# Moving two sets of loads in a one-core encoder layer: the memories behind the mixer's first output weights, the attention projection's loads behind those of the heads

## The chip, the core and the metric

The kernel runs on one NeuronCore of a Trainium2 chip. The core has a matrix engine (TensorE; PE in the profile, and PEld for its weight loads), a vector engine (VectorE; DVE), a scalar engine (ScalarE; ACT), a general engine (GpSimd; POOL) and a queue engine (SyncE; SP) that does little but issue DMA transfers between the device's memory and the on-chip buffer. The metric is device microseconds of the whole program, from launch to end, as a median of several runs.

## What is computed

One layer of an encoder, for two groups of tokens that share their weights: a sample group S (512 tokens) and a prompt group P (256 tokens), each token 1024 numbers wide, everything in fp32. The layer has four parts; each ends with a residual sum and a layer norm:

```python
x = layer_norm(DN_ALPHA * x + 0.5 * swiglu(x, ffn1_w_gu, ffn1_w_down), ...)
x = layer_norm(DN_ALPHA * x + parallel_mixer(x, ...), ...)          # ends with  merged @ w_out
x = layer_norm(DN_ALPHA * x + memory_cross_attention(x, mem, w_q, w_kv, w_o), ...)
x = layer_norm(DN_ALPHA * x + 0.5 * swiglu(x, ffn2_w_gu, ffn2_w_down), ...)

def memory_cross_attention(x, mem, w_q, w_kv, w_o):
    q = (x @ w_q).reshape(B, T, 4, 256)
    k, v = jnp.split(mem @ w_kv, 2, axis=-1)                        # mem: 256 vectors for each group
    s = jnp.einsum('bthd,bmhd->bhtm', q, k) * (256 ** -0.5)
    o = jnp.einsum('bhtm,bmhd->bthd', jax.nn.softmax(s, axis=-1), v)
    return o.reshape(B, T, 1024) @ w_o
```

The change touches the seam between the mixer and the attention, and the end of the attention.

## The kernel before, in words

**Products in three parts.** Every fp32 operand is split by `split` (L83) into a high part, copied by ScalarE (L84), and a low part, the difference, made by VectorE (L85). A product is then three matmuls (L103, L104, L105: high by high, high by low, low by high).

**Weights.** `load_w` (L87) loads 128x1024 of weights (512 KB) through the SP queue (L93) into a `raw` tile, and splits it into `wh` and `wl`. The pool has three `raw` places and five of each of `wh` and `wl`. A load therefore waits until one of the three raw places has been split, and a split until one of the five weight places has been used up.

**The seam.** The mixer's last matmuls are those of its second branch (`pt<-oT`, traced by `branch`, L1019, with VectorE's `put_gla`, L1032). Then `attention` (L1082) begins, in this order of the program:

- It opens three pools, among them `mem` for the split memories `mh` and `ml`. That pool takes over space of pools that the mixer's end has just closed.
- L1099 to L1104, four times: both groups' memories, two transfers of 256 KB (L1102), into a `raw` tile of the same three places; then a split into `mh` and `ml`. The memories are first used much later, by `keys_values` (L1110).
- `tok_out` (L1055) for the mixer's output product: six groups of token tiles and halves of the columns, three groups for the first half, then the same three for the second. A group uses four weight tiles, each loaded the first time it is needed (L1063), and makes matmuls named `to`. Between the weights of the first groups `tok_out` can call hooks: it takes one list of functions from `hooks` after each weight tile (L1070).
- Norms, transposes (`lt`), the keys and values into DRAM (`kd`, `vd`), and the queries, which are made with a seven-product scheme (`products`, L488) from sums of the inputs held in a pool `sums`, staged in a pool `qs` and stored to DRAM (`qd`) by ScalarE's queue (L1228).

**The heads.** `fetch` (L1200) loads q (1536 KB), k and v (1024 KB each) of a head through SP (L1212). Heads 0 and 2 have their q and k in a pool `even`, heads 1 and 3 in a pool `odd`; each pool has one place for q and one for k, so q and k of head 2 wait until the scores of head 0 have been made, and those of head 3 until the scores of head 1 have. There are two places for v. `odd` is opened after `qs` and `sums` have been closed and takes their space. For each head there are `scores` (matmuls `sc`, then the softmax), `probs_T` (transposes `pT`) and `values` (matmuls `ov`).

**The projection.** A second `tok_out` (L1320) multiplies by `w_xo`. It loads eight weight tiles (L93; all but the first five go into a pool that is opened by a hook), and its hooks make the last head's values, bring the residual back (`x2_back`, L1303: six loads of 512 KB, L1305) and load the norm's parameters. After that comes the second feed-forward part.

**What sets the order.** The engines run their instructions in a fixed order that is made when the kernel is compiled. The scheduler goes through a planned time; of the instructions that it holds ready at a moment, it puts the one that stands earliest in the program next on its engine. On the chip each engine then keeps that order: an SP transfer that waits holds up all SP transfers behind it, whether they could go or not. `tc.issue_after(ins)` adds a rule for the order alone: what is traced in the block on the engine of `ins` comes behind `ins` on that engine. It adds no wait.

Of the kernel before, what the change touches and what calls it, by code (L numbers as in the profile page):

```python
# [7 lines left out]
F32 = mybir.dt.float32  # L8
# [33 lines left out]
S = Stream("S", TS, 0)  # L42
P = Stream("P", TP, TS)
# [12 lines left out]
def _encoder(ctx, tc, nc, io, out, dbg):  # L56
# [6 lines left out]
    def psum(name):  # L63
        return pp.tile([128, 512], F32, tag="ps", name=name)
# [13 lines left out]
    def nid(p):  # L78
        uid[0] += 1
        return f"{p}{uid[0]}"  # L80


    def split(hi, lo, src, lo_eng=None):  # L83
        nc.scalar.activation(hi, src, AF.Copy)  # L84
        (lo_eng or nc.vector).tensor_tensor(lo, src, hi.bitcast(F32), op=ALU.subtract)  # L85

    def load_w(src, lo_eng=None, pool=None, in_parts=False, extra=1):  # L87

        raw = wp.tile([128, 1024], F32, tag="raw", bufs=3, name=nid("raw"))
        h = (pool or wp).tile([128, 1024], F32R, tag="wh", bufs=extra if pool else 5, name=nid("wh"))  # L90
        l = (pool or wp).tile([128, 1024], F32R, tag="wl", bufs=extra if pool else 5, name=nid("wl"))
        def part(a, b):
            nc.sync.dma_start(raw[:, a:b], src[:, a:b])  # L93
            split(h[:, a:b], l[:, a:b], raw[:, a:b], lo_eng)

        halves = [(h[:, c:c + 512], l[:, c:c + 512]) for c in (0, 512)]
        if in_parts:
            return halves, part
        part(0, 1024)
        return halves  # L100
# [20 lines left out]
    def tok_mm(ps, w, kk, lh, ll, start, stop, cols=slice(0, 512)):  # L121
        mm3(ps, lh, ll, w[kk][0][:, cols], w[kk][1][:, cols], start, stop)
# [57 lines left out]
    def to_T(s, t):  # L180

        tc_ = slice(t * 128, (t + 1) * 128)
        A = glob["acc"][:, s.t0 + t, :]
        for kq in range(2):
            ps = psum(nid("lt"))
            for j in range(4):
                c = (kq * 4 + j) * 128
                nc.tensor.transpose(ps[:, j * 128:(j + 1) * 128], A[:, c:c + 128], ident[:])  # L188
            p3 = ps[:].rearrange("p (a b) -> p a b", b=128)
            split(xh[s.name][:, kq * 4:kq * 4 + 4, tc_], xl[s.name][:, kq * 4:kq * 4 + 4, tc_], p3)  # L190
# [14 lines left out]
    def add_acc(s, t, half, ps, first, cols=slice(0, 512)):  # L205
        A = glob["acc"][:, s.t0 + t, half * 512 + cols.start:half * 512 + cols.stop]
        if first:
            nc.vector.scalar_tensor_tensor(A, A, ALPHA, ps, ALU.mult, ALU.add)
        else:
            nc.vector.tensor_tensor(A, A, ps, op=ALU.add)  # L210
# [844 lines left out]
    def tok_out(src, order, lhs, after, hooks=(), more=None):  # L1055


        hooks, ws = list(hooks), {}
        for gi, (s, ts, half) in enumerate(order):
            pss = [psum(nid("to")) for _ in ts]  # L1060
            for kp in range(4):
                if (kp, half) not in ws:
                    ws[kp, half] = load_w(src[kp, half], pool=more() if more and len(ws) >= 5 else None, extra=3)  # L1063
                for x, t in enumerate(ts):
                    tcs = slice(t * 128, (t + 1) * 128)
                    for kk in range(2):
                        k = 2 * kp + kk
                        lh, ll = lhs(s, k, tcs)
                        tok_mm(pss[x][:], ws[kp, half], kk, lh, ll, k == 0, k == NK - 1)
                if hooks:  # L1070
                    for f in hooks.pop(0):
                        f()
            for x, t in enumerate(ts):
                add_acc(s, t, half, pss[x][:], True)
            for f in after.get(gi, ()):
                f()
# [5 lines left out]
    def attention():  # L1082
# [3 lines left out]
        x2 = dp.tile([128, 6, D], F32, name="x2")  # L1086
# [5 lines left out]
        def opened(name, side="left"):  # L1092
            stack[name] = ExitStack()
            return stack[name].enter_context(tc.tile_pool(name=name, bufs=1, reuse_waits="tile", side=side))

        mp, sg, lp = opened("mem", "right"), opened("stage"), opened("lnx")
        mh, ml = [mp.tile([128, NK, 512], F32R, name=f"m{p}") for p in "hl"]

        for c in range(4):  # L1099
            r = wp.tile([128, 1024], F32, tag="raw", bufs=3, name=nid("raw"))  # L1100
            for n, s in enumerate(STREAMS):
                nc.sync.dma_start(r[:, n * 512:n * 512 + 512], io[f"mem{s.name}"][c])  # L1102
            split(*[m[:, 2 * c:2 * c + 2, :].rearrange("p k (s t) -> p k s t", s=2) for m in (mh, ml)],
                  r[:].rearrange("p (s k t) -> p k s t", s=2, k=2))  # L1104
# [30 lines left out]
        def norms(s, ts, i, gb, dst):  # L1135
            def f():
                for t in ts:
                    norm(s, t, gb, i)
                    nc.sync.dma_start(dst[:, s.t0 + t, :], glob["acc"][:, s.t0 + t, :])
            return f  # L1140

        def ln_params(pool, i):
            return load_ln(lambda nm: pool.tile([128, 512], F32, tag="gb", bufs=4, name=nm), i)

        pending.append(keys_values())
        gb = ln_params(lp, 1)
        groups = [(S, (0, 1)), (S, (2, 3)), (P, (0, 1))]
        tok_out(io["w_mix_out"], [g + (half,) for half in range(2) for g in groups], merged,
                {3 + n: [norms(s, ts, 1, gb, x2)] for n, (s, ts) in enumerate(groups)})
        to_T(S, 0)  # L1150
        to_T(S, 1)
        fill(FILL[0])
# [29 lines left out]
        for k in range(4):  # L1182
            fill(FILL[2])
            a = []
# [10 lines left out]
        stack["mem"].close()  # L1195

        ev, od = opened("even", "right"), None
        tl = {}

        def fetch(h, parts):  # L1200
            pool = ev if h % 2 == 0 else od
            for p in parts:
                if p == "q":
                    t = pool.tile([128, 2, 2, TT], F32R, tag="q", bufs=1, name=nid("q"))
                    src = qd[:, 2 * h:2 * h + 2]
                elif p == "k":
                    t = pool.tile([128, 2, 2, 512], F32R, tag="k", bufs=1, name=nid("k"))
                    src = kd[:, 2 * h:2 * h + 2]
                else:
                    t = od.tile([128, 4, 2, 256], F32R, tag="v", bufs=2, name=nid("v"))  # L1210
                    src = vd[:, h]
                nc.sync.dma_start(t[:].bitcast(F32), src)  # L1212
                tl[p, h] = t

        fetch(0, "k")
        qs = opened("qs", "right")
        for h in range(4):
            g1, x, u1, u2 = products(ws)
            for b, parts in ((1, (u1, u2)), (0, (g1, x))):
                t = qs.tile([128, 2, TT], F32R, tag="qst", bufs=2, name=nid("qst"))  # L1220
# [48 lines left out]
        def probs_T(h, s):  # L1269
            p = od.tile([128, 2, 2, s.T], F32R, tag="p" + s.name, bufs=1, name=nid("p"))  # L1270
            pr[h, s] = p
            for m in range(2):
                ps = psum(nid("pT"))
                for t in range(s.nt):
                    c = t * 256 + m * 128
                    nc.tensor.transpose(ps[:, t * 128:(t + 1) * 128], es[h, s][:, c:c + 128], ident[:])
                split(p[:, m, 0, :], p[:, m, 1, :], ps[:, :s.T])

        def values(h, s):

            v, p = tl["v", h], pr[h, s]
            m0 = 0 if s is S else 2
            for b in range(2):
                ps = psum(nid("ov"))[:, :s.T]
                c = slice(b * 128, (b + 1) * 128)
                for m in range(2):
                    mm3(ps, v[:, m0 + m, 0, c], v[:, m0 + m, 1, c], p[:, m, 0, :], p[:, m, 1, :], m == 0, m == 1)
                split(xh[s.name][:, 2 * h + b, :], xl[s.name][:, 2 * h + b, :], ps)
# [14 lines left out]
        def x2_back(ts):  # L1303
            for t in ts:
                nc.sync.dma_start(glob["acc"][:, t, :], x2[:, t, :])  # L1305

        late = {}
# [8 lines left out]
        def ln3(s, ts):  # L1316
            return lambda: norms(s, ts, 2, late["gb"], x3)()

        a, b, c = groups
        tok_out(io["w_xo"], [a + (0,), b + (0,), a + (1,), b + (1,), c + (0,), c + (1,)], merged,  # L1320
                {2: [ln3(*a)], 3: [ln3(*b)], 4: [lambda: [to_T(S, t) for t in range(4)]], 5: [ln3(*c)]},
                [[lambda: probs_T(3, S), lambda: probs_T(3, P)], [lambda: values(3, S), lambda: x2_back((0, 1))],
                 [lambda: values(3, P)], [reopen]], lambda: late["pool"])
        for nm in ("late", "stage"):
            stack[nm].close()

# [187 lines left out]
```

## Time and profile before

| what | value |
|---|---|
| median of 3 runs | 1799.23 us (1796.19 to 1800.26) |
| the profiled execution | 1797.84 us, of it a span of 1796.1 us from first to last instruction |
| PE busy | 1751.1 us, 97% of the span |
| DVE busy, ACT busy | 1267.2 us (71%), 753.8 us (42%) |
| POOL busy | 38.7 us (2%) |
| moved by DMA | 271.96 MB, a mean of 151 GB/s |

The two timeline slices (of forty) in which PE is not busy for nine tenths or more, apart from the last, are its 21st and its 27th, both with 6 tenths. The 21st, from 898 to 943 us, is the seam between mixer and attention, and the 27th, from 1167 to 1212 us, the first heads. A busy time says how long an engine had an instruction; the waits say what released an engine that had none, and the chain of waits follows the program back from its end through whatever came last at each step. "To landing" is the time from the issue of a transfer to its arrival. The granted clock is the share of TensorE's full clock.

### The profile page before, as it was taken

What the parts mean: (1) busy time and instruction counts of PE and PEld (TensorE: products, weight loads), DVE (VectorE), ACT (ScalarE), POOL (GpSimd) and SP (SyncE); (2) the same over time, 40 slices, a digit from 0 to 9 for tenths busy, and PEclk for the clock granted to TensorE, in tenths of its full rate; (3) what the DMA queues carried; (4) which work ended last, traced back from release to release, by engine and by line L of the source; (5) the groups of instructions that cost most, each with busy time, mean ns of one, the idle gap of its engine ahead of it and who ended that gap; (6) DMA issues with size and microseconds to landing.
All of it is one profiled execution on the core that took longest, in us unless ns stands there. A gap on an engine that the chain in (4) does not pass through costs nothing.

```text
span 1796.1 us, 24825 instructions
## 1 busy us (share of the span) xinstructions
PE 1751.1 (97%) x9518; PEld 1607.2 (89%) x9518; DVE 1267.2 (71%) x2191; ACT 753.8 (42%) x1303; POOL 38.7 (2%) x72
## 2 busy tenths in 40 slices
PE   9999999999999999999969999969999999999998
PEld 9999999888899999888868888958899999998886
DVE  8777777597677564778663976644987777776866
ACT  6444444453145555655232244432234444444531
POOL 0000000000100000000000000020000000000002
PEclk9999999999999999999989999989999999999999
DMA  5333332686333334111553445682214333337951
GB/s 200 133 124 117 125 133 91 248 313 233 112 111 113 130 123 152 59 48 47 163 203 115 147 168 191 248 340 80 106 59 157 128 110 119 131 103 280 338 190 71
DMA packets 106038, 271.96 MB, mean 151 GB/s; under 512 B 10400, under 2 KB 32672, under 8 KB 104384
## 3 DMA queue, kind: packets, MB, share of 16 engines
q1 hardware_dynamic: 91776, 239.97, 38.9%
q10 hardware_dynamic: 14144, 30.41, 4.5%
q8 instruction: 74, 1.21, 0.3%
q14 instruction: 44, 0.36, 0.1%
HBM read 206.12 MB, written 64.23 MB: 151 GB/s over the span
## 4 chain that ended last, share of the span: by engine, by line
PE 92%; DVE 3%; DMA 3%; ACT 1%; issue 1%; SPq 0%; ACTq 0%; DVEq 0%
PE px L472 24%; PE dn L283 13%; PE py L472 12%; PE pz L472 6%; PE pt L103 5%; PE pt L104 5%; PE pt L105 5%; PE to L103 3%; PE to L104 2%; PE to L105 2%; PE dn L103 2%; PE dn L104 2%; PE dn L105 2%; PE pp L472 1%; DMA k<-kd 1%; PE lt L188 1%
## 5 line engine op out<-in xcount | busy, mean ns | idle before, releaser
L84 ACT ACTIVATE wh<-raw 128x512 fp32r<-128x512 f32 (+2 forms) x281 | 221.0, 789 | 280.4 <-PE to L105 91.0
L85 DVE TENSOR_TENSOR wl<-raw,wh 128x512 fp32r<-128x512 f32 (+2 forms) x281 | 249.1, 889 | 105.2 <-ACT wh L84 104.9
L283 PE MATMUL dn<-wh,ao 128*128 128x512 f32 x600 | 185.5, 389 | 0.0
L283 PEld LDWEIGHTS dn<-wh,ao 128*128 128x128 f32 x600 | 112.6, 188 | 23.4
L103 PE MATMUL pt<-xh,wh 128*128 128x512 f32 (+2 forms) x384 | 129.9, 338 | 0.0
L104 PE MATMUL pt<-xl,wh 128*128 128x512 f32 (+2 forms) x384 | 129.3, 337 | 0.0
L105 PE MATMUL pt<-xh,wl 128*128 128x512 f32 (+2 forms) x384 | 128.9, 336 | 0.0
L84 ACT ACTIVATE wh<-tt 128x512 fp32r<-128x512 f32 x156 | 94.1, 626 | 71.9 <-PE px L472 60.4
L283 PE MATMUL dn<-wl,ao 128*128 128x512 f32 x300 | 116.7, 389 | 0.0
L85 DVE TENSOR_TENSOR wl<-tt,wh 128x512 fp32r<-128x512 f32 x156 | 104.3, 687 | 3.0 <-ACT wh L84 2.2
L472 PE MATMUL px<-xh,wh 128*128 128x384 f32 x280 | 93.6, 334 | 0.0
L472 PE MATMUL px<-xh,wl 128*128 128x384 f32 x280 | 93.6, 334 | 0.0
L472 PE MATMUL px<-xl,wh 128*128 128x384 f32 x280 | 93.5, 334 | 0.0
L103 PE MATMUL to<-wh,xh 128*128 128x512 f32 x192 | 76.1, 397 | 14.3 <-ACT wh L84 14.3
L549 DVE SCALAR_TENSOR_TENSOR h<-sil,sum 128x384 f32<-128x384 f32 x78 | 43.5, 558 | 54.7 <-ACT sil L548 54.7
L103 PEld LDWEIGHTS pt<-xh,wh 128*128 128x128 f32 x384 | 72.7, 189 | 7.4 <-issue 0.5
L105 PEld LDWEIGHTS pt<-xh,wl 128*128 128x128 f32 x384 | 72.7, 189 | 6.4
L104 PEld LDWEIGHTS pt<-xl,wh 128*128 128x128 f32 x384 | 72.7, 189 | 6.3 <-issue 0.2
L104 PE MATMUL to<-wl,xh 128*128 128x512 f32 x192 | 75.9, 395 | 0.0
L105 PE MATMUL to<-wh,xl 128*128 128x512 f32 x192 | 75.7, 394 | 0.0
L84 ACT ACTIVATE ao<-sr 128x768 fp32r<-128x768 f32 x50 | 41.9, 844 | 67.7 <-issue 24.8
L548 ACT ACTIVATE sil<-sum 128x384 f32<-128x384 f32 x39 | 20.5, 526 | 111.3 <-DVE sum L484 111.3
(404 smaller groups left out, 4792.7 us busy)
## 6 DMA issues: line engine op xcount, KB each, us to landing
raw<-in_ffn_gu_dram SPq DMA_DIRECT2D x84, 512.0 KB, 3.5
raw<-in_ffn_dn_dram SPq DMA_DIRECT2D x64, 512.0 KB, 5.4
raw<-in_w_mix_dram SPq DMA_DIRECT2D x32, 512.0 KB, 3.4
sr<-sspill SPq DMA_DIRECT2D x32, 384.0 KB, 5.2
sspill<-hs SPq DMA_DIRECT2D x56, 192.0 KB, 1.9
hspill<-hq SPq DMA_DIRECT2D x12, 768.0 KB, 3.7
hr<-hspill SPq DMA_DIRECT2D x24, 384.0 KB, 6.2
x<-acc SPq DMA_DIRECT2D x18, 512.0 KB, 2.8
```

Of the source, the lines that this page charges most:

```text
L84: nc.scalar.activation(hi, src, AF.Copy)
L85: (lo_eng or nc.vector).tensor_tensor(lo, src, hi.bitcast(F32), op=ALU.subtract)
L103: nc.tensor.matmul(o, lh, rh, start=start, stop=False)
L104: nc.tensor.matmul(o, lh, rl, start=False, stop=False)
L105: nc.tensor.matmul(o, ll, rh, start=False, stop=stop)
L188: nc.tensor.transpose(ps[:, j * 128:(j + 1) * 128], A[:, c:c + 128], ident[:])
L283: nc.tensor.matmul(ps[t][:], l, r[:, o], start=start and k == 0 and m == 0, stop=stop and k == 1 and m == 2, skip_group_check=True)
L472: nc.tensor.matmul(ps, l[:, c], r[:, k, :], start=st and n == 0, stop=sp_ and n == 2, skip_group_check=True)
L548: nc.scalar.activation(sil[:], g, AF.Silu)
L549: ins = nc.vector.scalar_tensor_tensor(h32[:, half * HT:(half + 1) * HT], sil[:], -0.5, u, ALU.mult, ALU.mult)
```

## The change

The loop over the four memory tiles becomes a function `memory(c)`, called from hooks of the first `tok_out`: its `hooks` are four empty lists and then one call each, so that `memory(0)` to `memory(3)` are traced after the four weights of the second group's first half, instead of ahead of `tok_out`.

The second `tok_out` is traced within `tc.issue_after` of the last `fetch`'s transfer (the v of head 3). All that it and its hooks issue on SP comes behind that transfer on the SP queue: eight loads of `w_xo`, six of the residual, the norm's parameters, and the stores of the norms' results. Nothing else is changed, and no instruction is added or removed.

```diff
         mh, ml = [mp.tile([128, NK, 512], F32R, name=f"m{p}") for p in "hl"]
-
-        for c in range(4):
+        def memory(c):
+
             r = wp.tile([128, 1024], F32, tag="raw", bufs=3, name=nid("raw"))
             for n, s in enumerate(STREAMS):
                 nc.sync.dma_start(r[:, n * 512:n * 512 + 512], io[f"mem{s.name}"][c])
...
         tok_out(io["w_mix_out"], [g + (half,) for half in range(2) for g in groups], merged,
-                {3 + n: [norms(s, ts, 1, gb, x2)] for n, (s, ts) in enumerate(groups)})
+                {3 + n: [norms(s, ts, 1, gb, x2)] for n, (s, ts) in enumerate(groups)},
+                [[]] * 4 + [[lambda c=c: memory(c)] for c in range(4)])
...
-        tl = {}
+        tl, last_fetch = {}, [None]
...
-                nc.sync.dma_start(t[:].bitcast(F32), src)
+                last_fetch[0] = nc.sync.dma_start(t[:].bitcast(F32), src)
...
         a, b, c = groups
-        tok_out(io["w_xo"], ...)
+        with tc.issue_after(last_fetch[0].ins):
+            tok_out(io["w_xo"], ...)
```

More of the change, by code (lines that the diff above doesn't have):

```diff
@@ L1319, in attention @@
         a, b, c = groups
[L1320 to L1323, printed above, removed]
+        with tc.issue_after(last_fetch[0].ins):
+            tok_out(io["w_xo"], [a + (0,), b + (0,), a + (1,), b + (1,), c + (0,), c + (1,)], merged,
+                    {2: [ln3(*a)], 3: [ln3(*b)], 4: [lambda: [to_T(S, t) for t in range(4)]], 5: [ln3(*c)]},
+                    [[lambda: probs_T(3, S), lambda: probs_T(3, P)], [lambda: values(3, S), lambda: x2_back((0, 1))],
+                     [lambda: values(3, P)], [reopen]], lambda: late["pool"])
         for nm in ("late", "stage"):
```

## The prediction
> **What bounds the kernel now.** First the page, then TensorE's own waits (us in total, times, longest).
>
> ```profile
> PE 1751.1 (97%) x9518; PEld 1607.2 (89%) x9518; DVE 1267.2 (71%) x2191; ACT 753.8 (42%) x1303; POOL 38.7 (2%) x72
> ```
> ```profile
> PE sc L103 <- DMA k<-kd: 17.4, 1, 17.4
> PE to L103 <- ACT wh L84: 14.3, 1, 14.3
> ```
>
> TensorE is the bound. Of its 45 us without work (the span of 1796.1 less 1751.1) two waits make 31.7. The change is about just these two, so each is read in its stage.
>
> The first, in the timelines of SP, of ACT and DVE, and of PE (start, us, engine, what; in brackets the idle time before and what ended it):
>
> ```profile
> 870.03 0.33 SPq L1102 DMA_DIRECT2D raw<-in_memS_dram  x1
> ...
> 886.75 0.33 SPq L1102 DMA_DIRECT2D raw<-in_memS_dram  x1
> ...
> 934.99 1.22 SPq L93 DMA_DIRECT2D raw<-in_w_mix_out_dram  x2
> ```
> ```profile
> 931.27 2.95 ACT L84 ACTIVATE mh<-raw 128x1024 fp32r<-128x1024 f32 x3
> 932.37 3.50 DVE L85 TENSOR_TENSOR ml<-raw,mh 128x1024 fp32r<-128x1024 f32 x3 [0.56 <-ACT mh L84]
> 942.44 1.06 ACT L84 ACTIVATE wh<-raw 128x1024 fp32r<-128x1024 f32 x1 [4.40 <-DMA raw<-in_w_mix_out_dram]
> 943.55 0.79 PE L103 MATMUL to<-wh,xh 128*128 128x512 f32 x1 [14.28 <-ACT wh L84]
> ```
>
> Three memory tiles (the first and the third load are shown) take the three raw places from 870 to 887 us and keep them until their splits at 931, after the mixer's last branch. Only at 934.99 can the first weights of the output product be loaded. TensorE ends the branch at 929.27 and waits 14.28 us.
>
> The second, on SP, in SP's waits and on PE:
>
> ```profile
> 1152.85 10.38 SPq L93 DMA_DIRECT2D raw<-in_w_xo_dram  x3
> ...
> 1167.54 0.81 SPq L1305 DMA_DIRECT2D acc<-x  x2
> 1171.74 0.82 SPq L1212 DMA_DIRECT2D q<-qd  x2
> 1172.61 0.49 SPq L1212 DMA_DIRECT2D k<-kd  x1
> 1174.52 0.32 SPq L1212 DMA_DIRECT2D v<-vd  x1
> 1176.39 0.32 SPq L1212 DMA_DIRECT2D k<-kd  x1
> ```
> ```profile
> SPq L1212 <- PE sc L105: 3.3, 1, 3.3
> ```
> ```profile
> 1171.43 0.28 PE L105 MATMUL sc<-k,q 128*128 128x256 f32 x1
> ```
>
> SP is occupied with the projection until 1168.4, then waits 3.3 us for the scores of head 0. Only a q that takes the place of head 0's has to wait for those: so the first q is head 2's, and q and k of head 1, which TensorE needs next, stand behind it. Head 0's scores end at 1171.7; the first k, head 1's, is issued at 1172.61, and TensorE goes on 17.4 us after it stopped.
>
> Then what the two stretches leave behind. The windows give length, PE busy (instructions), PEld, DVE, ACT, POOL where there are any, PEclk, DMA share, GB/s. The first two are of the `to` instructions alone, the next two of `sc`, the others of all.
>
> ```profile
> 943.50:949.40 5.90, 5.81 (x13) 4.17 (x14) 0.00 (x0) 0.50 0.59 201
> 949.50:955.40 5.90, 5.90 (x27) 4.85 (x27) 0.00 (x0) 0.99 0.75 226
> ```
> ```profile
> 1189.00:1191.80 2.80, 2.70 (x13) 2.73 (x14) 0.00 (x0) 0.00 (x0) 0.50 1.01 427
> 1200.50:1203.30 2.80, 2.73 (x23) 2.80 (x24) 0.69 (x1) 0.08 (x1) 1.00 0.99 420
> ```
> ```profile
> 901.90:908.90 7.00, 7.00 (x43) 6.14 (x42) 0.00 (x0) 0.00 (x0) 0.00 (x0) 1.00 0.99 396
> 909.00:932.00 23.00, 20.26 (x117) 17.45 (x115) 22.74 (x48) 8.99 (x17) 0.00 (x0) 1.00 0.36 108
> 934.00:1013.00 79.00, 69.41 (x298) 56.92 (x299) 44.50 (x101) 14.84 (x15) 0.00 (x0) 0.90 0.37 123
> 1171.70:1189.10 17.40, 0.01 (x1) 0.03 (x1) 2.44 (x9) 2.57 (x12) 2.94 (x3) 0.59 1.00 422
> 1198.50:1220.80 22.30, 22.17 (x160) 20.33 (x159) 17.03 (x44) 14.47 (x44) 7.61 (x7) 1.00 0.67 258
> ```
>
> After each wait the granted clock is 0.50: 13 matmuls in 5.90 us against 27, so 13 should take 2.84, and 3.06 us are lost; after the second wait 13 in 2.80 us against 23, 1.22 lost.
>
> **The change, part by part.** No instruction is added; all prices are waits.
>
> *Memories.* Traced later, their loads find the output weights ahead of them: three weights take the raw places from 870, and the splits of these free them for the rest. A split also needs a weight place; one falls free with each weight of the branch that has been used. DVE has no work at all from 901.9 to 908.9, which holds the first splits (1.06 us on ACT; on DVE 1.2, a third of the 3.50 above). From 909 to 932 DVE is busy 22.74 of 23: three more splits there would end its last work 3.6 us later, near 935.5. But the first group needs that last operand only with its fourth weight, 36 matmuls of 0.22 or 8 us after its start at 929.3. So TensorE goes on almost at once. Residue: from 0 to 6.8 (all weights split behind DVE's last work: ready at 933.0, so 3.7 idle, and some 3 of half clock). I take 0.5, near the lower end because of the empty 7 us.
>
> The memories' own four splits (4.2 us of ACT, 4.7 of DVE) and their eight transfers on SP go into the output product. From 934 to 1013 ACT is free for 64 of 79 us and DVE for 34, the DMA share is 0.37, and the memories are first used at 1013.6:
>
> ```profile
> L103 PE MATMUL pt<-mh,wh x64: 392/392/484, 1013.6 to 1061.3; 128*128 128x512 f32 x64
> ```
>
> So they cost nothing; without that cover it would be 1.2 us a split. **Gain 14.28 + 3.06 − 0.5 = 16.8.**
>
> [...]
>
> *Projection behind the heads.* SP then holds only fetches between head 0's q and the last v. Those of head 1 need the space of the sums, whose last use is:
>
> ```profile
> L472 PE MATMUL py<-qS4h,wl x16: 334/334/343, 1115.5 to 1162.4; 128*128 128x384 f32 x16
> ```
>
> At the 422 GB/s of the window above, q (1536 KB) takes 3.7 us and k 2.5. A transfer of 512 KB with little beside it needs 3.4 (the row below), 1.2 of it for its bytes, so 2.2 are fixed.
>
> ```profile
> raw<-in_w_mix_dram SPq DMA_DIRECT2D x32, 512.0 KB, 3.4
> ```
>
> Issued by 1162.8, q and k land by 1171.2, before head 0's scores end. Head 2's, issued at 1171.7, need 2.2 + 3.7 + 2.5, and 1.9 for a query store of 768 KB beside them: 1182.0. TensorE wants them one head after 1171.55, and a head takes 10.15 (from the first matmul of head 2's scores to that of the projection are two heads):
>
> ```profile
> 1200.57 0.28 PE L103 MATMUL sc<-k,q 128*128 128x256 f32 x1
> ...
> 1220.88 0.40 PE L103 MATMUL to<-wh,xh 128*128 128x512 f32 x1
> ```
>
> That is 1181.7. Residue 0 to 4 (head 1's v slipping ahead, 2.5, and half clock); I take 1.0, nearer to the 0.3 that this sum gives.
>
> All this supposes that head 1's q now stands ahead of head 2's, which is the scheduler's matter. The order of before shows that it held both ready at nearly the same moment: head 2's q went first, but head 1's q, k and v went before head 2's k. What made head 1 ready so late must come at the end of the queries, whose pools it takes over. There stood, on ACT:
>
> ```profile
> 1167.74 1.06 ACT L84 ACTIVATE wh<-raw 128x1024 fp32r<-128x1024 f32 x1 [1.13 <-PE px L472]
> 1168.70 0.47 ACT L1223 ACTIVATE qst<-px 128x384 fp32r<-128x384 f32 x1
> ```
>
> a split of a projection weight in front of the last query stage. It goes away with the loads, and its half on DVE too, while head 0's scores stay where they are: so I take the order as turned.
>
> *Its price.* The projection's weights, five of them split early before, now start behind the last v:
>
> ```profile
> 1210.92 0.32 SPq L1212 DMA_DIRECT2D v<-vd  x1
> ```
>
> That is 9.96 us ahead of the first `to`. v lands in 4.7, the first weight 1.2 behind it; 0.4 for issuing and 2.3 for the split make 8.6, so 1.4 are to spare. Six residual loads ahead of it would add 7.4: 6 us late, 9 with half clock. I take 0.5, since two weights stand ahead of the first residual in the program. All fourteen loads (1.2 each) have landed 22 us after v's issue; the first residual is needed 26 after it. The new splits fall among the softmaxes, where DVE has 5 of 22 us free. **Gain 17.39 + 1.22 − 1.0 − 0.5 = 17.1.**
>
> Sum 33.9. The profiled execution took 1797.84 (the span and 1.74 around it), so 1763.9; the median lies 1.4 above it: **1765.3**.
>
> **The rivals.** A measurement of this kernel can tell about 3.6 us (0.2%) from no change.
>
> *The order of the fetches stays:* head 2's q still waits for head 0's scores, with head 1 behind it. Then only the traffic ahead of them is gone: the last weight and two residuals, 1.5 MB or 3.7 us off the second wait instead of 17: 1778. For it: nothing in the change names these two fetches. Against it: the close readiness. Chance 0.16.
>
> *The first weights are late for `to`,* 3 to 9 us as above: 1771. For it: DVE's full stretch. Against it: the 1.4 to spare. Chance 0.08.
>
> *The memories keep their raw places,* and the first wait stays; the change doesn't do what it says: 1782. Against it: the weights now stand ahead in the program and need nothing but the same place. Chance 0.04.
>
> *Slower:* raw places that stay empty while the projection is held back are taken by loads of the second feed-forward part, which nothing holds back. The eight weights then pass through one place, one after the other. If a weight takes p from issue to freed place, the first half is done 4p + 2.7 after v's issue instead of 26.4, and the second half takes 4p instead of two groups' 21.8: 8p − 45.5 lost. It eats the gain of 33.9 from p = 9.9. Loads of `w_xo` took, from issue to landing:
>
> ```profile
> DMA to landing us min/median/max: 3.5/7.1/8.9
> ```
>
> With 2.3 for the split p is up to 11.2, which loses 44: 1809. Against it: those loads stand later in the program. Chance 0.03.
>
> **How the numbers follow.** Forecast 0.69 (1760 to 1769), kept fetch order 0.16 (1776 to 1783), late weights 0.08, kept memories 0.04, slower 0.03. The range runs from the lowest run less all gains without residue and a little for what ACT and DVE no longer have in the queries' stage (1758) to the end of the kept order (1783). Faster 0.95, within 0.2% 0.02 (the slower rival near its break-even), slower 0.03.
>
> **What would show it.** Right: loads of `w_mix_out` on SP at 870 to 887; `to` within 1 us of the last `pt<-oT`; no half clock in either stage; q and k of head 1 issued by 1163 less the first gain; the first `w_xo` right behind the last v. Wrong: a `q` that waits for `sc` ahead of head 1's, a new wait of `to` for `wh` after the heads, or feed-forward loads ahead of `w_xo`.

## The result, and the profile after

| | median of the runs | range | runs |
|---|---|---|---|
| before | 1797.82 us | 1796.19 to 1800.26 | 4 |
| after | 1776.87 us | 1775.70 to 1778.86 | 4 |

The ratio is 0.9883, with a 95% interval of 0.9866 to 0.9901: faster by 20.95 us, where 33.9 were forecast. The time lies within the range, but at the place of a rival (the order of the fetches stays, 1778), and 11.6 us above the forecast of 1765.3. The profiled execution of after took 1777.92 us, with a span of 1776.1.

First the page's busy times and TensorE's waits in the kernel after (us in total, times, longest):

```profile
PE 1749.7 (99%) x9518; PEld 1607.4 (91%) x9518; DVE 1266.4 (71%) x2191; ACT 753.2 (42%) x1303; POOL 38.6 (2%) x72
```
```profile
PE sc L103 <- DMA k<-kd: 12.6, 1, 12.6
PE py L472 <- ACT acc L477: 1.8, 1, 1.8
```

The wait of `to` is gone, and no new one stands in the list; that of `py` was 1.6 us before. The wait of `sc` for a k is still there and has lost only 4.8 of its 17.4 us. (Lines of the attention stand one or two further down in the kernels below: the fetch is L1213 in after, the query store L1229.)

**The seam.** SP's timeline after, and TensorE's over the same border:

```profile
869.85 0.33 SPq L93 DMA_DIRECT2D raw<-in_w_mix_out_dram  x1
...
886.57 0.33 SPq L93 DMA_DIRECT2D raw<-in_w_mix_out_dram  x1
...
902.82 0.42 SPq L93 DMA_DIRECT2D raw<-in_w_mix_out_dram  x1
...
910.21 0.38 SPq L1102 DMA_DIRECT2D raw<-in_memS_dram  x1
```
```profile
928.87 0.28 PE L105 MATMUL pt<-oT,wl 128*128 128x256 f32 x1
928.99 0.39 PE L103 MATMUL to<-wh,xh 128*128 128x512 f32 x1
```

The raw places that the memories took are taken by weights, at the same three moments, and a fourth weight follows at 902.82. The first `to` comes 0.12 us behind the last matmul of the branch, at the usual pace. The windows (length, PE busy and count, PEld, DVE, ACT, POOL, PEclk, DMA share, GB/s) over the stretches that the prediction relied on:

```profile
909.00:932.00 23.00, 23.00 (x131) 19.91 (x130) 22.88 (x46) 9.90 (x17) 0.00 (x0) 1.00 0.43 133
934.00:1013.00 79.00, 79.00 (x357) 65.27 (x356) 58.78 (x147) 17.72 (x21) 0.00 (x0) 1.00 0.45 156
```

TensorE has no idle moment in either and the clock is 1.00. Before, it was busy 20.26 of 23 in the first, and 69.41 of 79 at a mean clock of 0.90 in the second. The memories' loads now go out between 910.21 and 935.97, their splits run from 932.8 to 943.5, and neither costs TensorE anything.

**The heads.** SP's timeline, the SP waits that go with it, and TensorE's stop:

```profile
1114.61 41.98 SPq L1213 DMA_DIRECT2D q<-qd  x3
1156.65 0.43 SPq L1213 DMA_DIRECT2D k<-kd  x1
...
1180.84 10.49 SPq L1213 DMA_DIRECT2D v<-vd  x2
1191.39 1.17 SPq L93 DMA_DIRECT2D raw<-in_w_xo_dram  x2
```
```profile
SPq L1213 <- DMA qd<-qst: 36.6, 2, 27.9
SPq L1213 <- PE sc L105: 12.8, 1, 12.8
```
```profile
1155.49 0.28 PE L105 MATMUL sc<-k,q 128*128 128x256 f32 x1
...
1168.35 0.55 PE L103 MATMUL sc<-k,q 128*128 128x256 f32 x1 [12.58 <-DMA k<-kd]
```

The three q in the first row are those of heads 0, 2 and 1, in this order: the second waits 27.9 us for its own query stores to land and then 12.8 more until the scores of head 0 are done at 1155.77. For these 40.7 us nothing else moves on SP, and only then do q and k of head 1 go. The projection's loads are gone from in front (the first `w_xo` stands behind the last v, as the change says), but the fetch they were to make room for isn't the next one. Three windows show the stop and its echo:

```profile
1155.90:1159.30 3.40, 0.00 (x0) 0.00 (x0) 2.04 (x8) 1.78 (x8) 2.63 (x3) 1.00 0.78 241
1159.50:1168.30 8.80, 0.00 (x0) 0.00 (x0) 0.00 (x0) 0.00 (x0) 0.05 (x1) 0.50 1.00 423
1168.50:1173.00 4.50, 4.50 (x22) 4.50 (x23) 0.86 (x2) 0.73 (x3) 0.00 (x0) 0.50 1.01 428
```

No work for 12.58 us, while the DMA engines move 423 GB/s for most of it; then 22 matmuls at half clock in 4.65 us (the first starts at 1168.35), which at the pace of the prediction's full-clock row for `sc` (23 in 2.73) take 2.61: 2.0 lost.

So the sum of what went away is 14.28 + 3.06 at the seam and (17.39 + 1.22) − (12.58 + 2.0) = 4.0 at the heads: 21.3 us. The medians differ by 20.95, the spans of the two profiled executions by 20.0. One thing works against the gain in the profiled execution of after, far from both stages: behind the 1.82 us in which `py` waits for `acc`, the granted clock is 0.50 from 1097.9 to 1101.4. There 12 matmuls take 3.74 us and the 12 ahead of the wait took 2.07, so 1.7 us are lost that before did not lose. What has to be explained is why the second term is 4.0 and not 17.1.

### The profile page after: what moved, and what is told of

Read it like the earlier page. It is cut to its first block, busy times and chain, and to the rows that moved or that the text cites. A ratio compares the mean times of both kernels' runs of the same rounds, so it can differ in the third digit from the quotient of the medians.

```text
span 1776.1 us, 24813 instructions
## 1 busy us (share of the span) xinstructions
PE 1749.7 (99%) x9518; PEld 1607.4 (91%) x9518; DVE 1266.4 (71%) x2191; ACT 753.2 (42%) x1303; POOL 38.6 (2%) x72
## 4 chain that ended last, share of the span: by engine, by line
PE 95%; DVE 2%; DMA 2%; ACT 1%; issue 0%; SPq 0%; ACTq 0%; DVEq 0%
PE px L472 24%; PE dn L283 13%; PE py L472 12%; PE pz L472 6%; PE pt L104 5%; PE pt L103 5%; PE pt L105 5%; PE to L103 2%; PE to L105 2%; PE to L104 2%; PE dn L103 2%; PE dn L104 2%; PE dn L105 2%; PE pp L472 1%; PE lt L188 1%; PE V L105 1%
```

## The experiments

The theory: both parts do what they say, and the second one is worth little only because head 2's q still goes ahead of head 1's on SP. A rival: q of head 1 couldn't have gone any earlier, because the space that it takes over wasn't free. Each run is compared with runs of the kernel before on the same chip (a median of 1797.55 us of 10 runs for the first four, 1797.14 of 7 for the last three).

| kernel | median (range), us | ratio to before (95%) |
|---|---|---|
| e1, the memories' part alone | 1781.58 (1780.98 to 1782.48) | 0.9910 (0.9893 to 0.9926) |
| e2, the projection's part alone | 1791.91 (1790.12 to 1795.15) | 0.9968 (0.9957 to 0.9979) |
| e3, after, and head 1 fetched first | 1763.61 (1762.83 to 1766.08) | 0.9812 (0.9797 to 0.9826) |
| e4, e1 and head 1 fetched first | 1778.59 (1777.79 to 1780.39) | 0.9894 (0.9879 to 0.9909) |
| e5, before, memories in other raw tiles | 1782.34 (1781.21 to 1784.49) | 0.9915 (0.9900 to 0.9930) |
| e6, after, and a pool for the probabilities | 1763.26 (1762.71 to 1763.97) | 0.9808 (0.9793 to 0.9822) |
| e7, e1 and a pool for the probabilities | 1770.45 (1769.86 to 1774.48) | 0.9853 (0.9834 to 0.9872) |

### Each part alone (e1, e2)

e1 is the kernel before with the diff's first part only:

```diff
-        for c in range(4):
+        def memory(c):
...
-                {3 + n: [norms(s, ts, 1, gb, x2)] for n, (s, ts) in enumerate(groups)})
+                {3 + n: [norms(s, ts, 1, gb, x2)] for n, (s, ts) in enumerate(groups)},
+                [[]] * 4 + [[lambda c=c: memory(c)] for c in range(4)])
```

> The memories' part alone; the projection's loads stay where they were. Theory (the two waits are separate, and the first is made by the raw places alone): the first wait of 14.3 us and its half clock of some 3 us go, the second stays at 17.4 us: 1797.8 - 17.2 = 1780.6 us. Rival (the parts help each other, since the earlier stage also moves the traffic of the later one): the second wait changes by over 2 us, and the time lies outside 1779 to 1782.

Measured: 1781.58, and in TensorE's waits the first is gone and the second as it was:

```profile
PE sc L103 <- DMA k<-kd: 17.4, 1, 17.4
```

The memories' part is worth 16.0 us of medians, where the seam's wait and half clock had made 17.3. Part of the difference stands at the heads: the wait there is as long as before, but half clock goes on for 4.2 us behind it and not for 2.8.

e2 is the kernel after with the memories left where they were (the same lines turned round).

> The projection's part alone; the memories are loaded ahead of the output product as before. Theory (the order of the two q loads stays, only traffic ahead of them goes): first wait 14.3 us as before, second 12 to 14 us, 1797.8 - 3.8 = 1794 us. Rival (the order turns when the stage lies elsewhere): second wait under 3 us, 1781 us.

Measured: 1791.91, 5.6 below before. TensorE's waits:

```profile
PE to L103 <- ACT wh L84: 12.7, 1, 12.7
PE sc L103 <- DMA k<-kd: 12.6, 1, 12.6
```

The second wait is the 12.6 us of after. The first was expected as before (14.3) and is 1.6 shorter, though nothing of the change is near it. From the issue of the first weight load to its split are 6.4 us in e2 (934.57 to 941.01), and in the profiled execution of before 7.5 (934.99 to 942.44). So 1.0 of the 1.6 is the same transfer landing sooner. These are two single executions; why it did was not followed. By what is left to each part when the other is there, the projection's part takes 5.6 us off before and 4.7 off e1. It makes room on SP, but not the room that head 1 needs.

### The order of the two fetches (e3, e4)

e3 is the kernel after, with one rule more: on SP, q and k of the head after next come behind k of head 1. The rule adds no wait; on the SP queue it moves the one q of head 2 behind q and k of head 1 (and v of head 0).

```diff
         fetch(1, "qk")
+        k1 = last_fetch[0]
         fetch(0, "v")
...
             if h < 2:
-                fetch(h + 2, "qk")
+                with tc.issue_after(k1.ins):
+                    fetch(h + 2, "qk")
```

> The changed kernel with one more rule: the q and k of head 2 (and of head 3) stand behind the k of head 1 on SP. Theory (order): head 1's q is issued as soon as the sums are used up, near 1147 us of the changed kernel's span, lands before head 0's scores end, and the wait of 12.6 us and its half clock of some 2 go; 0 to 2 us remain for head 2: 1761 to 1764 us. Rival (space): head 1's loads cannot go before the last query store has landed (1155.9), so only the 3.7 us of head 2's q are gained: wait 8.9 us, 1773 us.

Measured: 1763.61. TensorE's wait for the k, SP's timeline, and the last query store on ACT's queue:

```profile
PE sc L103 <- DMA k<-kd: 0.4, 1, 0.4
```
```profile
1112.84 27.03 SPq L1213 DMA_DIRECT2D q<-qd  x2
1141.62 0.32 SPq L1213 DMA_DIRECT2D k<-kd  x1
```
```profile
1151.07 0.33 ACTq L1229 DMA_DIRECT2D qd<-qst  x1
```

The second q of the first row, head 1's, is issued at 1139.5, 11.5 us before the last query store is even issued and some 15 before head 0's scores end. So on the chip neither the space nor the data kept it back in after; only the q that stood ahead of it in the queue did. The rival falls, and the order alone is worth 13.3 us on top of after.

e4 asks whether the order is enough without the projection held back: e1 with the same rule.

> The memories' part and head 1 ahead of head 2, but the projection's loads not held back. Theory (the projection's loads hold up SP and the rings, whatever the order of the heads): head 1's q is issued only behind the projection's and the residual's loads, near 1151 us, with some 1.5 MB ahead of it; a wait of 8 to 10 us remains: 1772 to 1774 us. Rival (the order of the heads is all): as e3, 1761 to 1764 us.

Measured: 1778.59 with a wait of 15.1 us, a miss. SP's timeline, and the page of transfers issued from 1148.5 to 1156 us (KB each, median us from issue to landing):

```profile
1152.65 0.33 SPq L93 DMA_DIRECT2D raw<-in_w_xo_dram  x1
1153.09 1.24 SPq L1213 DMA_DIRECT2D q<-qd  x1
1154.42 0.45 SPq L1213 DMA_DIRECT2D k<-kd  x1
```
```profile
acc<-x SPq DMA_DIRECT2D x3, 512.0 KB, 8.3
qd<-qst ACTq DMA_DIRECT2D x2, 768.0 KB, 8.4
q<-qd SPq DMA_DIRECT2D x1, 1536.0 KB, 13.6
raw<-in_w_xo_dram SPq DMA_DIRECT2D x2, 512.0 KB, 8.7
k<-kd SPq DMA_DIRECT2D x1, 1024.0 KB, 14.8
```

Head 1 is first here too, yet its q stands on SP behind the projection's loads until 1153.09, and once issued it shares the DMA engines with three residuals, two weights and two query stores: 4096 KB beside the 2560 KB of q and k. At the 423 GB/s of the windows above all of it takes some 16 us; the k lands at 1169.2 (1154.42 + 14.8), where TensorE goes on. The rule of order alone takes 3.0 us off e1, the held-back projection alone 4.7, and both together 18.0 (1781.58 to 1763.61): **each of these two is worth most of its gain only when the other is there.** The rule puts head 2 behind head 1, but here it doesn't bring head 1 ahead of the projection; e7 below turns the order in another way and fares better.

### What holds the memories' places (e5)

The kernel before, with the memories' raw tiles taken from a staging pool (`sg`) and no longer from the three places that the weights use; loads and splits keep their place in the program.

```diff
-            r = wp.tile([128, 1024], F32, tag="raw", bufs=3, name=nid("raw"))
+            r = sg.tile([128, 1024], F32, tag="stg", bufs=2, name=nid("raw"))
```

> The kernel before, with one edit: the memories' raw tiles come from the stage pool instead of the three raw places; they keep their place in the program, ahead of the output product. Theory (it was the raw places that made the first wait): as with the memories traced later, no first wait, second wait as before: 1781 to 1782 us. Rival (it is the place in the program, that is the memories' splits ahead of those of the weights): a first wait of 3 to 14 us stays, 1785 to 1797 us.

Measured: 1782.34, as e1 (1781.58), and its only long wait of TensorE is the second:

```profile
PE sc L103 <- DMA k<-kd: 17.3, 1, 17.3
```

So with the raw places left to the weights the wait is gone, though the memories still stand ahead in the program. But the order on the engines did not stay as it was. SP's timeline and ACT's in e5, and the wait on SP of a memory's load in before (840 to 1010 us):

```profile
902.32 0.42 SPq L93 DMA_DIRECT2D raw<-in_w_mix_out_dram  x1
...
932.85 0.33 SPq L1102 DMA_DIRECT2D raw<-in_memS_dram  x1
```
```profile
938.04 2.26 ACT L84 ACTIVATE mh<-raw 128x1024 fp32r<-128x1024 f32 x2 [6.84 <-DMA raw<-in_memP_dram]
```
```profile
SPq L1102 <- DVE ml L85: 5.1, 1, 5.1
```

In the trace of before the raw places are the last link: the first weight's split waits 4.40 us for its transfer (942.44, in the prediction's rows), and that transfer is issued behind the fourth memory's, which waits 5.1 us on SP until a memory's split frees a raw place. In e5 the memories' loads and splits come behind those of the weights, on SP and on ACT. So sharing the raw places made the first wait; how much of it would stay with weights loaded early but split behind the memories, no run tried.

### Why the scheduler keeps head 2 first (e6, e7)

The pool `odd` holds q, k and v of the odd heads, but the probabilities `p` too, and it takes over space both of `sums` and of the query staging `qs`. After e3 the theory is that the scheduler counts a pool as ready only when all that it takes over is free, here the last query store's landing. In after that store is issued, and takes to land:

```profile
1152.61 0.33 ACTq L1229 DMA_DIRECT2D qd<-qst  x1
```
```profile
qd<-qst ACTq DMA_DIRECT2D x1, 768.0 KB, 3.3
```

It lands at 1155.9, and the scores whose end makes head 2 ready end at 1155.77. In e6 the probabilities get a pool of their own, opened where `qs` was, so that `odd` takes over nothing of `qs`:

```diff
-        stack["qs"].close()
         stack["sums"].close()
         od = opened("odd")
+        stack["qs"].close()
+        pb = opened("probs", "right")
...
-            p = od.tile([128, 2, 2, s.T], F32R, tag="p" + s.name, bufs=1, name=nid("p"))
+            p = pb.tile([128, 2, 2, s.T], F32R, tag="p" + s.name, bufs=1, name=nid("p"))
...
-            for nm in ("odd", "even"):
+            for nm in ("odd", "probs", "even"):
```

> The changed kernel with no rule for the heads' order, but with the probabilities' tiles in a pool of their own, so that the pool of head 1's q, k and v takes over the space of the sums alone and nothing of the query stage. Theory (the scheduler counts a pool as free only when all that it takes over is, here the landing of the last query store, though the loads themselves wait only for what they overlap): head 1's loads come ahead of head 2's of themselves, second wait gone, as in the run with head 1 first: 1762 to 1765 us. Rival (the scheduler prefers head 2 for another reason): wait 12.6 us as in the changed kernel, 1777 us.

Measured: 1763.26, with no wait of `sc` in TensorE's list. SP's timeline:

```profile
1113.25 26.93 SPq L1213 DMA_DIRECT2D q<-qd  x2
1141.94 0.32 SPq L1213 DMA_DIRECT2D k<-kd  x1
...
1154.58 0.32 SPq L1213 DMA_DIRECT2D q<-qd  x1
```

With no rule of order at all, head 1 goes first, within 0.4 us of the moments of e3, and head 2's q follows at 1154.58. So what kept head 1 back in the plan was that `odd` shared space with the query staging. (That the plan waits for the store's landing, and not only for its issue, no run shows.) This is the fastest kernel of the study, level with e3.

e7 is e1 with the same pool and the projection not held back.

> The memories' part and the probabilities' own pool, but the projection's loads not held back: five of the eight stand ahead of head 1's on SP, the rest and three residual loads behind. Theory (what counts is how much stands ahead of head 1): the fifth load waits for a raw place until some 1146 us, so head 1's loads go then, with 0.5 to 1.3 MB ahead of them, and land near 1158, against 1154.4 for the end of head 0's scores: a wait of 2 to 4 us and at most 2 of half clock: 1765 to 1769 us. Rival (any projection load ahead spoils it, as when only the order of the heads was set): wait over 10 us, 1775 to 1779 us. Second rival (the projection's part is not needed at all): no wait, 1762 to 1765 us.

Measured: 1770.45, above what was expected, and not by the wait that was expected: `sc` waits for nothing, but `ov` does. TensorE's wait, ACT's timeline, the last query stage on DVE and, from the transfers, the store:

```profile
PE ov L103 <- ACT p L84: 5.2, 1, 5.2
```
```profile
1150.25 1.06 ACT L84 ACTIVATE wh<-raw 128x1024 fp32r<-128x1024 f32 x1 [1.13 <-PE px L472]
...
1151.21 0.47 ACT L1224 ACTIVATE qst<-px 128x384 fp32r<-128x384 f32 x1
...
1154.46 0.33 ACTq L1229 DMA_DIRECT2D qd<-qst  x1
...
1165.35 1.08 ACT L84 ACTIVATE p<-pT 128x512 fp32r<-128x512 f32 x2 [6.19 <-DMA qd<-qst]
```
```profile
1153.88 0.55 DVE L1228 TENSOR_TENSOR qst<-px,qst 128x384 fp32r<-128x384 f32 x1
```
```profile
qd<-qst ACTq DMA_DIRECT2D x1, 768.0 KB, 10.8
```

Now it is the first `p`, in the space of `qs`, that waits for the last query store to land. A projection weight is split in front of the last query stage on ACT (1150.25), which starts 0.9 us later than in e6 (1151.21 against 1150.27). On DVE the stage comes 3.1 us later (1153.88 against 1150.80): the weight's low part stands ahead of it there (1151.34), and then work on head 0's scores (two `mx` reductions from 1152.48). So the store goes at 1154.46, 3.1 us later than in e6 (1151.39). By then head 2's q has been issued, 0.2 us ahead of it, with k and v right behind, and it needs 10.8 us to land, where e6's store needed 3.9. First SP in e7 and the clock after the stop (a window as above), then the store in e6:

```profile
1154.25 0.32 SPq L1213 DMA_DIRECT2D q<-qd  x1
```
```profile
1165.50:1172.10 6.60, 6.10 (x16) 4.91 (x17) 3.39 (x7) 3.56 (x10) 0.92 (x1) 0.50 1.02 421
```
```profile
1151.39 0.33 ACTq L1229 DMA_DIRECT2D qd<-qst  x1
```

The 5.2 us, and about half of the 6.2 us that TensorE then works at half clock, come to the 8.3 us between the spans of e7 and e6 (1769.1 and 1760.8; 7.2 between the medians). This is read from the trace; no run tried it by itself. It says that the held-back projection has a second use: it keeps the splits of its weights out of the end of the queries. Still, e7 is 11.1 us below e1, where the rule of e4 gave 3.0: with the pool, head 1's q goes at 1140.0, ahead of the projection's last loads, and not at 1153.09.

## Why the prediction was partly right

**The direction and the range held; the forecast did not.** The range held only because its upper end was drawn to take in a rival with a chance of 0.16, and that rival came. By its own steps:

- *TensorE is the bound, and two waits make most of its idle time.* Right. With both gone (e6) the span is 1760.8, 35.3 below before.
- *The first wait goes, 16.8.* Right, and a little better: the residue is 0, where 0.5 was taken and up to 6.8 allowed. It was 17.3 by the waits and the clock, 16.0 by the medians of e1. e5 shows the cause that the step named, the sharing of the raw places, though with the order of the splits turned as well.
- *The memories' own splits and transfers cost nothing.* Right: 79.00 of 79 us busy.
- *Head 1 could be fetched before head 0's scores end, with a residue of 0 to 4.* Right about the chip: e3 has 0.4 left, where 1.0 was taken. It could go earlier than the last use of the sums, which the step took for the limit (1162.8 less the first gain of some 17, so near 1146): e3 issues it at 1139.5.
- *The price of the projection behind the heads, 0.5, with 1.4 to spare.* Nothing measured: no wait of `to` stands in the lists of after, e3 or e6. In after the first `w_xo` is issued 9.6 us ahead of the first `to` (1200.96), and a window around it is all but full:

```profile
1182.00:1204.00 22.00, 21.89 (x150) 19.61 (x149) 17.46 (x42) 15.41 (x43) 6.50 (x6) 1.00 0.75 293
```

- *"So I take the order as turned."* **This is the step that failed.** Its ground was that the end of the queries would come earlier against head 0's scores, once a projection weight's split no longer stood in front of the last query stage. That did happen. In the kernel before the last store stands on ACT's queue at

```profile
1171.95 0.33 ACTq L1228 DMA_DIRECT2D qd<-qst  x1
```

which is 0.2 us behind the end of head 0's scores (1171.7); in after it is issued 3.2 us ahead of that end (1152.61 against 1155.77). But the step took the end of the queries' work for the moment at which head 1 is ready. e6 shows that `odd` was held by the staging it takes over, and e7 that such space is free only when the store has landed (the first `p` waits 6.19 us for it there), in after 3.3 us behind its issue, so 0.1 behind the scores. Of the 17.1 us that the step was to open the way for, 4.0 came. That the scheduler's plan had the two in the same order and as close as the chip shows is argued, not shown.
- *The rival "the order stays: 1778"* described just this, with q of head 2 waiting for head 0's scores and head 1 behind it, and priced it with "only the traffic ahead of them is gone", 3.7 us. Measured: 4.0 by waits and clock, 4.7 by medians against e1. Its chance of 0.16 looks low, though one outcome can't show that: the trace of before spoke of "nearly the same moment", and for a tie a shift by 3 us is no proof while the step's own reach, the landing of a 768 KB store, is as long.

The forecast for the turned order, 1765.3, is what e3 and e6 measured within 2.1 us (1763.61, 1763.26); of the residues in it (0.5 for the first wait, 1.0 for the second), e3 shows 0.4 at the second wait, and e6 shows none.

## What to carry to other kernels

When a change is to let a transfer go earlier, find out which transfer is put next on its queue, and name the last event on which that choice hangs. Here the scheduler held a pool back for space that it took over, though the tiles in question (q and k of head 1) could go some 15 us earlier on the chip. Give late-freed space to the tiles that are needed late (here the probabilities), or fix the order by a rule; either was worth 13 us. And two gains on one queue are not a sum: on top of e1 the rule alone gave 3.0, the cleared queue alone 4.7, both 18.0. Turning the order at its cause, by the pool, gave 11.1 even without the cleared queue (e7).

## What the runs showed of the hardware

The price of a stop isn't only its length. The trace's record of the granted clock (its stretch at the program's end left aside) has half clock for 17.07 us after both stops of before (14.3 and 17.4 us long) and after the one long stop of e1 (17.4) and of e5 (17.3), for 13.65 in after (12.6), in e2 (12.7 and 12.6) and in e4 (15.1), and for 6.83 in e7 (5.2): five, four and two times 3.413, the length of the one short stretch in after (1097.938 to 1101.351). Over these nine stops it set in 2.8 to 4.6 us after TensorE stopped, and ended 2.8 to 6.2 after it went on. So the echo doesn't follow the length of the stop: 3.06 us were lost after 14.3 us in before, 1.22 after 17.4. TensorE was at work at half clock for up to 6.2 us after a stop (6.0 after the first of before, 6.2 in e7). No run here moved a stop on purpose, so what sets the length of the echo is not shown.

A short wait can have an echo too. The wait of `py` for `acc` was 1.82 us long in after and 1.79 in e5, and half clock of 3.41 us set in 2.2 and 2.6 us after TensorE had stopped, when it was already at work again. In the other seven profiled executions this wait was 1.6 to 1.7 us long and had no echo; so few cases give no threshold.

A transfer took longer to land where more was issued with it. The same 768 KB store landed after 3.3 us in after, 3.9 in e6 and 10.8 in e7. In e7 head 2's q was issued 0.2 us ahead of it, and k and v within 0.9 us behind it: 4352 KB in all, which at the 421 GB/s of the window there take 10.6 us.
